# Aligning ScalarE's instruction stream to a 256-slot block in a two-layer expert kernel

## The chip, the cores and the metric

The kernel runs on one core of a Trainium2 chip. A core has five engines, each with an instruction stream of its own: TensorE (PE in the profile; PEld is its weight load), VectorE (DVE), ScalarE (ACT), GpSimd (POOL) and SyncE (SP). Data moves between the chip's memory and the core's buffers by DMA, over 16 DMA engines that all queues share. The metric is the time of one execution on the device, in microseconds (us); smaller is better.

## What is computed

Eight experts each apply two dense layers with bias to 256 rows of their own:

```python
n_experts, capacity, hidden, expert_hidden = 8, 256, 512, 2048
h = np.matmul(x, w1) + b1[:, np.newaxis, :]
h = np.maximum(h, 0)
return (np.matmul(h, w2) + b2[:, np.newaxis, :]).astype(np.float32)
```

All inputs and the output are 32-bit floats in the chip's memory. `w1` and `w2` together are 64 MiB of the data that must be read.

## The kernel before

The five engines' programs are written out by hand, one function for each, inside one critical section (L396): nothing there is reordered, and the only order between engines is by semaphores.

**Loads.** `run_gpsimd` issues the weight loads, which convert to 16-bit floats on the way: `w1` of an expert in one transfer of 2 MB as it lands (L173), `w2` likewise (L183), in halves for the last two experts. Three buffers stand for each (`NW = 3`), so a load of expert e + 3 waits until TensorE has done with expert e. `run_sync` issues the first loads of `x` and `b1` (L148, L150), turns the landing of weights into counts that TensorE can wait for (L155, L161), and issues the output of the last two experts. GpSimd also loads the small row `b2` (L187) and writes out the other results (L206).

**Compute.** TensorE walks `E + LAG = 11` steps in a loop over registers (L324). Step s does layer 1 of expert s (L344: 16 blocks j of 128 hidden columns, four matmuls each, into the four buffers `ph`) and layer 2 of expert s - 3 (L359 for the bias, L374 for 16 x 2 matmuls, into `po`). Its loop body is a few dozen instructions, run again and again.

**ScalarE** (`run_scalar`), by contrast, is straight code, one instruction for each piece of work, in this order:

- it waits until VectorE has transposed a pattern (L210, on `turned_steps`), copies four pieces of it into the identity matrix `ident` (L214, with a table load ahead of the first), which TensorE needs for its first transposes of `x` (L291);
- it waits for `x` of experts 2 and 3 and casts it (L218);
- it waits for the transposed `b1` and, for each expert and each j, applies bias and relu from `ph` to `hT` (L115, 128 in all); each one frees a `ph` buffer for TensorE (`ph_free`);
- from step 3 on, after the relus of a step, it copies results out of `po` (L127, 22 in all), which frees `po` for TensorE.

**VectorE** makes the transposes of `x` and `b1` (L235, L247, L266), casts the first two experts' `x`, copies what TensorE transposed (L241), and takes half of the copies from `po` of the last two experts.

At the end of the section the engines meet, SyncE issues the last output (L404) and waits for all of it. Ahead of the section each engine has a few instructions of the frame and one branch into the section (put down to L437).

Of the kernel before, what the change touches and what calls it, by code (L numbers as in the profile page):

```python
# [10 lines left out]
def kernel(  # L11
# [90 lines left out]
    def relu(e, j):  # L102
        rows = rows_of(e)
        R = x_rows(e)
        to, columns = hT[:, e % NH, j, :], ph[j % NPH][:, 0:T]
        if T // rows > R:
            m = T // rows // R
            to = to.rearrange("p (m r i) -> p m r i", m=m, r=R)
            columns = columns.rearrange("p (r i m) -> p m r i", r=R, m=m)
        else:  # L110
            m = R // (T // rows)
            to = to.rearrange("p (r i m) -> p r i m", m=m, i=rows // m)
            columns = columns.rearrange("p (m r i) -> p r i m", m=m, i=rows // m)
        at = j * B + e * nB + nB - 1
        return nc.scalar.activation(  # L115
            out=to, in_=columns, func=relu_of, bias=b1T[:, at : at + 1], scale=1.0)

    def result(e):

        if e in GROUP_OF:  # L120
            first, n = GROUP_OF[e]
            return grouped[first], (e - first) * (P // n), P // n, n
        return pair[e - (E - 2)], 0, P, 1

    def evict(e, lo, hi, k, copy):
        t, at, rows, split = result(e)
        return copy(  # L127
            out=t.rearrange("p (tb s) h -> p tb s h", s=split)[at : at + rows, lo:hi, k, :],
            in_=po[k * rows : (k + 1) * rows, e % 2, lo:hi, 0:H])

    def scalar_from(e):

        return 0 if e in GROUP_OF else nTB // 2
# [73 lines left out]
                s_out[first], 16)  # L207
    def run_scalar():
        a = nc.scalar
        a.wait_ge(turned_steps, 1)  # L210
        marks = {0: (ph_free, NPH), 1: (po_free_a, 1), nB - 1: (made_ident, 1)}
        for b in range(nB):
            part = slice(b * B, (b + 1) * B)
            ins = a.copy(out=ident[part, part], in_=steps_turned[part, :, 0])  # L214
            if b in marks:
                ins.then_inc(*marks[b])
        a.wait_ge(s_xg[2], 16)
        a.copy(out=x16[2], in_=x32[2]).then_inc(cast, 1)  # L218
        a.wait_ge(b1T_full, 1)
        for step in range(E + LAG):  # L220
            if step < E:
                for j in range(nJ):
                    a.wait_ge(ph_full, nJ * step + j + 1)
                    relu(step, j).then_inc(ph_free, 1)
            if step >= LAG:
                e = step - LAG
                a.wait_ge(po_full, ENDS * (e + 1))
                for k in range(result(e)[3]):
                    ins = evict(e, scalar_from(e), nTB, k, a.copy)
                ins.then_inc(po_free_a, 1)  # L230
# [165 lines left out]
    with tc.tile_critical(sync_engine=mybir.EngineType.SP, no_gpsimd_drain=True):  # L396
        run_gpsimd()
        run_sync()
        run_scalar()
        run_vector()  # L400
        run_tensor()
        nc.sync.wait_ge(po_free_a, 1 + E)
        nc.sync.wait_ge(po_free_d, 1 + E)
# [38 lines left out]
```

## Time and profile before

| what | value |
|---|---|
| median of 3 runs | 180.88 us (180.86 to 181.0) |
| the profiled execution's own time | 180.9 us |
| its span, from the first to the last instruction of the kernel | 179.1 us |
| around the span | 1.8 us |
| TensorE busy | 130.5 us (73%) |
| ScalarE busy | 82.0 us (46%), 156 instructions |
| VectorE busy | 40.2 us (22%) |
| data moved by the core's DMA | 40.98 MB, 229 GB/s |
| granted TensorE clock, mean | 0.964 of full speed |

How to read the views: a row of the timeline has a start, a length, the engine, the line and the operation, and how many instructions were merged (x4); in brackets stands the idle time of the engine before it and what ended it. A row of the groups has busy time and the mean of one instruction in ns, then idle time. A row of the DMA issues has how many there were, the size of each and the median time from issue to landing. A row of one source line has the shortest, median and longest duration in ns, then the first and the last start in us. In the queue part, q0 and q1 carry data and q14 carries the engines' program code. "issue" is time in which an engine waited for nothing that the profile shows. All times are counted from the span's start.

### The profile page before, as it was taken

The numbers are of one execution on the slowest core, as the hardware profiler recorded it, in microseconds if no ns is written. First come the engines' busy times: TensorE is split into PE (matmuls) and PEld (weight loads), VectorE is DVE, ScalarE is ACT, GpSimd is POOL, SyncE is SP. The second block draws the span as 40 slices with busy tenths as digits, with TensorE's granted clock in tenths as the row PEclk, the third lists the DMA queues.
The fourth block names the chain that finished last, engine by engine and source line by source line (L and its number), as shares of the span: only waits on it lengthen the run. The fifth ranks groups of instructions, "written<-read, shape, count | busy, mean of one in ns | idle before, by whom it ended". The sixth has DMA issues, their size and how long they took to land.

```text
span 179.1 us, 2849 instructions
## 1 busy us (share of the span) xinstructions
PE 130.5 (73%) x800; PEld 86.6 (48%) x800; DVE 40.2 (22%) x43; ACT 82.0 (46%) x156; POOL 13.2 (7%) x30
## 2 busy tenths in 40 slices
PE   0210695969879970899957995999669997999750
PEld 0200485858768430785436643774268433444310
DVE  0492299200000299992000000000000000001010
ACT  0500685877858126384089606890398212131010
POOL 7100003020010110001010001000200001002000
PEclk9999999999999998589999999699999999999996
DMA  5999999989989999998998999999899899999996
GB/s 194 267 249 302 212 198 234 231 179 234 236 187 220 238 209 201 234 223 187 234 234 183 227 234 198 212 234 220 190 234 234 183 227 205 210 225 209 318 454 252
DMA packets 3825, 40.98 MB, mean 229 GB/s; under 512 B 448, under 2 KB 464, under 8 KB 1008
## 3 DMA queue, kind: packets, MB, share of 16 engines
q0 software_dynamic: 3056, 37.76, 95.1%
q1 hardware_dynamic: 768, 3.21, 4.6%
q14 instruction: 1, 0.01, 0.0%
HBM read 71.39 MB, written 4.19 MB: 422 GB/s over the span
## 4 chain that ended last, share of the span: by engine, by line
DMA 44%; PE 23%; ACT 14%; another core or an unknown queue 11%; issue 4%; POOL 1%; SPq 0%; POOLq 0%
DMA w1sb<-in_w_dram 23%; PE ph L344 12%; DMA w2sb<-in_w_dram 12%; ACT hTsb L115 11%; PE po L374 10%; DMA b2sb<-in_b_dram 9%; ACT outg L127 2%; PE po L359 1%; POOL w1sb L173 0%; ACT pair L127 0%; POOL w2sb L183 0%; SPq L161 0%; SPq L155 0%; POOLq L437 0%
## 5 line engine op out<-in xcount | busy, mean ns | idle before, releaser
L344 PE MATMUL ph<-xTsb,w1sb 128*128 x512 | 67.7, 291 | 30.8 <-issue 15.1
L344 PEld LDWEIGHTS ph<-xTsb,w1sb 128*128 x512 | 58.6, 148 | 41.0 <-issue 38.5
L115 ACT ACTIVATE hTsb<-ph,b1T 128x256 f16<-128x256 f32 x128 | 56.7, 474 | 16.6 <-PE ph L344 16.2
L374 PE MATMUL po<-w2sb,hTsb 128*128 x256 | 56.8, 379 | 2.6 <-SPq L161 2.6
L374 PEld LDWEIGHTS po<-w2sb,hTsb 128*128 x256 | 25.0, 98 | 33.1 <-issue 5.7
L127 ACT COPY outg<-po 32x1024 f32<-32x1024 f32 (+1 forms) x20 | 20.1, 1005 | 43.7 <-PE po L374 43.5
L266 DVE STREAM_TRANSPOSE xTsb<-x 32x512 f16<-32x512 f16 (+1 forms) x32 | 31.0, 970 | 36.2 <-DMA x<-in_x_dram 29.0
L127 DVE COPY pair<-po 128x512 f32<-128x512 f32 x2 | 1.4, 692 | 88.5 <-PE po L374 88.5
L183 POOL DMA_DIRECT2D w2sb<-in_w_dram x10 | 5.3, 534 | 69.4 <-PE po L374 69.4
L173 POOL DMA_DIRECT2D w1sb<-in_w_dram x8 | 4.4, 551 | 66.6 <-PE ph L344 65.6
L291 PE MATMUL ph<-ident,x 128*128 128x128 f16 x16 | 1.9, 310 | 7.8 <-ACT ident L214 7.8
L127 ACT COPY pair<-po 128x512 f32<-128x512 f32 x2 | 1.2, 586 | 13.9 <-PE po L374 13.9
L218 ACT CAST x<-outg 128x2048 f16<-128x2048 f32 x1 | 1.9, 1899 | 11.5 <-DMA outg<-in_x_dram 11.5
L359 PE MATMUL po<-b2sb,ones 1*128 x16 | 4.8, 379 | 0.8 <-issue 0.7
L291 PEld LDWEIGHTS ph<-ident,x 128*128 128x128 f16 x16 | 1.6, 144 | 7.8 <-ACT ident L214 7.8
L247 DVE STREAM_TRANSPOSE b1T<-b1rows 32x512 f32<-32x512 f32 x4 | 4.1, 1020 | 0.1
L214 ACT ACT_TABLE_LOAD x1 | 1.3, 1283 | 5.4 <-DVE hTsb L235 5.4
L359 PEld LDWEIGHTS po<-b2sb,ones 1*128 1x128 f16 x16 | 1.4, 90 | 3.5 <-issue 3.2
L206 POOL DMA_DIRECT2D out_dram<-outg x2 | 1.1, 537 | 15.2 <-DMA w2sb<-in_w_dram 15.2
L235 DVE STREAM_TRANSPOSE hTsb<-hTsb 128x1024 f16<-128x1024 f16 x1 | 1.2, 1245 | 4.1 <-POOL hTsb L194 4.1
L241 DVE COPY xTsb<-ph 128x1024 f16<-128x1024 f16 x2 | 1.4, 692 | 2.5 <-PE ph L291 2.5
L238 DVE CAST x<-pair 128x1024 f16<-128x1024 f32 x2 | 1.3, 666 | 0.0
(11 smaller groups left out, 4.0 us busy)
## 6 DMA issues: line engine op xcount, KB each, us to landing
w1sb<-in_w_dram POOLq DMA_DIRECT2D x8, 2048.0 KB, 32.5
w2sb<-in_w_dram POOLq DMA_DIRECT2D x6, 2048.0 KB, 45.1
w2sb<-in_w_dram POOLq DMA_DIRECT2D x4, 1024.0 KB, 23.1
out_dram<-outg POOLq DMA_DIRECT2D x1, 2048.0 KB, 12.9
pair<-in_x_dram SPq DMA_DIRECT2D x2, 512.0 KB, 3.8
outg<-in_x_dram SPq DMA_DIRECT2D x1, 1024.0 KB, 16.9
x<-in_x_dram POOLq DMA_DIRECT2D x1, 1024.0 KB, 31.3
out_dram<-outg POOLq DMA_DIRECT2D x1, 1024.0 KB, 8.6
```

The lines of the kernel that those rows point to most:

```text
L115: return nc.scalar.activation(out=to, in_=columns, func=relu_of, bias=b1T[:, at : at + 1], scale=1.0)
L127: return copy(out=t.rearrange("p (tb s) h -> p tb s h", s=split)[at : at + rows, lo:hi, k, :], in_=po[k * rows : (k + 1) * rows, e % 2, lo ...
L173: g.dma_start(out=w1_sb[:, e % NW], in_=w1[e].rearrange("(p kc) m -> p kc m", kc=nKC)).then_inc(s_w1[e], 16)
L183: g.dma_start(out=w2_sb[:, e % NW, lo:hi], in_=src[:, lo:hi]).then_inc(s_w2[e, h], 16)
L218: a.copy(out=x16[2], in_=x32[2]).then_inc(cast, 1)
L241: v.tensor_copy(out=xT[:, e], in_=ph[2 + e].bitcast(fp16).rearrange("p (kc t) -> p kc t", kc=nKC),).then_inc(xT_full, 1)
L247: ins = v.transpose(out=b1T[b * B : (b + 1) * B, nB - 1 - b : nB - 1 - b + nJ * B], in_=b1_rows.rearrange("r (i j) -> r j i", j=nJ))
L266: ins = v.transpose(out=to[b * B : (b + 1) * B, :, :, half * B : (half + 1) * B], in_=src.rearrange("p r (i kc) -> p kc r i", kc=nKC))
L291: ins = t.transpose(out=pt[:, kc, r, :], in_=rows[:, kc, :], identity=ident)
L344: ins = t.matmul(out=ph[i][:, 0:T], lhsT=w1_cols(w1_j, i, kc), rhs=x_cols[kc], start=(kc == 0), stop=(kc == nKC - 1),)
L359: t.matmul(out=po_f[:, bass.ds(o + tb * 512, H)], lhsT=ones1, rhs=b2_sb[0:1, bass.ds(b_e, H)], start=True, stop=False, skip_group_check=True,)
L374: ins = t.matmul(out=po_f[:, bass.ds(o + tb * 512, H)], lhsT=hT_f[:, bass.ds(h_e + (j * T + tb * P), P)], rhs=w2_f[:, bass.ds(w_e + j * H, ...
```

## The change

One line is added at the head of ScalarE's program:

```diff
     def run_scalar():
         a = nc.scalar
+        a.addr_align(256, max_nops=0)
         a.wait_ge(turned_steps, 1)
         marks = {0: (ph_free, NPH), 1: (po_free_a, 1), nB - 1: (made_ident, 1)}
         for b in range(nB):
```

`addr_align` is a directive to the loader. When the program is loaded, the next instruction of that engine (here the wait at L210) is placed at a multiple of 256 instruction slots of the engine's stream, and the slots left free ahead of it are filled. With `max_nops=0` none of the filling is run: if there is any, its first slot is a branch to the placed instruction. The rest of ScalarE's program follows behind it, unchanged, and the other four engines' programs are the same.

## The prediction

> **What bounds the kernel now.** I read the page's head, its 40 slices and its queues first, to see which resource is full.
>
> ```profile
> span 179.1 us, 2849 instructions
> DMA  5999999989989999998998999999899899999996
> q0 software_dynamic: 3056, 37.76, 95.1%
> q1 hardware_dynamic: 768, 3.21, 4.6%
> q14 instruction: 1, 0.01, 0.0%
> ```
>
> The two data queues hold 95.1 + 4.6 = 99.7% of sixteen engines' time, and only the first and the last slices of the DMA line are below 8. The kernel streams its weights; compute runs beside that stream. The last line is the one this change is about: one packet of program code, printed as 0.01 MB, was read inside the span.
>
> Second, ScalarE's waits, since it is ScalarE's program that is laid out anew. The columns are: who waited for what, total us, times, longest.
>
> ```profile
> ACT outg L127 <- PE po L374: 43.5, 6, 7.3
> ACT hTsb L115 <- PE ph L344: 16.2, 29, 2.9
> ACT pair L127 <- PE po L374: 13.9, 2, 8.3
> ACT x L218 <- DMA outg<-in_x_dram: 11.5, 1, 11.5
> ACT L214 <- DVE hTsb L235: 5.4, 1, 5.4
> ```
>
> That is 90.5 us of idle time, and every entry names another engine or a load. No entry is put down to "issue", which is where an engine short of code would show. So nothing visible is there for a better layout to take away.
>
> Third, where that one code packet lies. The DMA view of the stretch from 46.3 to 46.8 us has it; the stretches before and after have no q14 row.
>
> ```profile
> q14 instruction: 1, 0.01, 4.0%
> ```
>
> Its time on an engine is 4.0% x 16 engines x 0.5 us = 0.32 us. Whose code is it? ScalarE is in new code at that time, while TensorE is in its third round of the loop at L344. VectorE, GpSimd and SyncE issue nothing new near it, so I take it for ScalarE's. The groups of ScalarE up to 46.39 us, and its two lone waits, tell how far it had come.
>
> ```profile
> L115 ACT ACTIVATE hTsb<-ph,b1T 128x256 f16<-128x256 f32 x43 | 19.3, 473 | 6.4 <-PE ph L344 6.3
> L218 ACT CAST x<-outg 128x2048 f16<-128x2048 f32 x1 | 1.9, 1899 | 11.5 <-DMA outg<-in_x_dram 11.5
> L214 ACT ACT_TABLE_LOAD x1 | 1.3, 1283 | 5.4 <-DVE hTsb L235 5.4
> L214 ACT COPY ident<-hTsb 32x32 f16<-32x32 f16 x4 | 1.0, 240 | 0.1
> L210 ACTq EVENT_SEMAPHORE  x1: 17/17/17, 5.3 to 5.3; - x1
> L223 ACTq EVENT_SEMAPHORE  x1: 17/17/17, 20.7 to 20.7; - x1
> ```
>
> 43 + 1 + 1 + 4 + 1 + 1 = 51 instructions of the section. So in the program of before a block edge lies some 51 slots into the section (an estimate: the sequencer may be a few ahead). What did crossing it cost? ScalarE's timeline on both sides, with an earlier row to compare:
>
> ```profile
> 33.46 1.78 ACT L115 ACTIVATE hTsb<-ph,b1T 128x256 f16<-128x256 f32 x4 [0.26 <-PE ph L344]
> 45.34 1.78 ACT L115 ACTIVATE hTsb<-ph,b1T 128x256 f16<-128x256 f32 x4 [0.28 <-PE ph L344]
> 47.39 1.78 ACT L115 ACTIVATE hTsb<-ph,b1T 128x256 f16<-128x256 f32 x4 [0.26 <-PE ph L344]
> ```
>
> Four relus take 1.78 us in all three rows, and the gaps are 0.26 to 0.28 us, ended by TensorE. The crossing cost nothing that can be seen.
>
> **The change part by part.** It adds a directive ahead of the wait at L210: filler up to the next multiple of 256 slots and, with no filler to be run, one branch over it. No wait, DMA or computation is added, removed or reordered; no other engine's code moves.
>
> *The branch.* ScalarE has one branch of its own in the trace, next to the others' here:
>
> ```profile
> L437 ACTq COMPARE_BRANCH  x1: 33/33/33, 0.8 to 0.8; - x1
> L437 PEldq COMPARE_BRANCH  x1: 174/174/174, 0.8 to 0.8; - x1
> 5.39 1.28 ACT L214 ACT_TABLE_LOAD   x1 [5.39 <-DVE hTsb L235]
> ```
>
> One more branch is 0.03 us by ScalarE's row, and 0.17 us by TensorE's as the far bound. It comes at 0.8 us, and ScalarE has nothing to do until VectorE's transpose ends at 5.3 us (the wait at L210). That wait hides 4.5 us, so the branch costs 0.
>
> *The code that it jumps to.* If the target has been read ahead, the jump is the branch alone. If it hasn't, ScalarE waits for a read. The trace of before has no such wait, so I bound it: from below 0.32 us, the code packet; from above the smallest loads' time to landing.
>
> ```profile
> pair<-in_x_dram SPq DMA_DIRECT2D x2, 512.0 KB, 3.8
> b1rows<-in_b_dram SPq DMA_DIRECT2D x1, 64.0 KB, 7.6
> b2sb<-in_b_dram POOLq DMA_DIRECT2D x1, 8.0 KB, 15.6
> 0.96 0.86 SPq L148 DMA_DIRECT2D pair<-in_x_dram  x2
> ```
>
> The first data is issued only at 0.96 us, so at 0.8 us a code read meets empty engines. The nearest row is the first one issued, 3.8 us for 512 KB; 0.8 + 3.8 = 4.6 us, still before 5.3. And there is a second cover behind the first:
>
> ```profile
> 7.76 1.89 PE L291 MATMUL ph<-ident,x 128*128 128x128 f16 x16 [7.76 <-ACT ident L214]
> 9.69 0.69 DVE L241 COPY xTsb<-ph 128x1024 f16<-128x1024 f16 x1 [0.16 <-PE ph L291]
> 19.23 1.90 ACT L218 CAST x<-outg 128x2048 f16<-128x2048 f32 x1 [11.53 <-DMA outg<-in_x_dram]
> 2.13 15.56 DMA b2sb<-in_b_dram
> 17.70 1.90 issue
> ```
>
> What ScalarE makes first (the identity) feeds TensorE's transposes and VectorE's copies, done at 9.69 + 0.69 = 10.4 us; in the chain that ended last TensorE then stands until the small load lands at 17.7 us. That leaves 7.3 us more. A stall at the jump would have to exceed 4.5 + 7.3 = 11.8 us to move the first matmul; I take 0.
>
> [...]
>
> *The code packet.* Where its edge moves from slot 51 to slot 0, the read of the block behind it moves from 46.4 us to about 0.8 us, from full engines to empty ones. All sixteen engines must finish each load, so at most its 0.32 us goes; an edge further on puts one back. I take 0, with -0.32 and +0.32 as ends.
>
> *The sum* against the profiled execution: 180.9 us = 179.1 of span + 1.8 around it, and the change 0 + 0 + 0. The median of the three times is 180.88, so the forecast is 180.9.
>
> **The rivals.** About 0.2% (0.36 us) is what a measurement of this kernel can tell from no change; a bare packet of 0.32 us stays below that.
>
> *A, forecast:* all of it is hidden, 180.9, within 180.6 to 181.2 by the packet's two ends. For it: waits without "issue", the crossing at 46.4 us for nothing, a cover of 11.8 us at the jump.
>
> *B, faster, in the end code.* What ScalarE runs after the last row of the profile lies in the 1.8 us around the span. The section has 8 + 128 + 22 = 158 instructions, five more close the program; from the old edge that end is 163 - 51 = 112 slots away, from the new one 163. If a block is shorter than 256 slots (0.01 MB is what one read brought), before has its next edge close behind the program's end, and the changed one hasn't. Bounds 0 and -1.8; I take half, -0.9: 180.0. Against it: nothing of that time is in any row.
>
> *C, slower, in the middle.* If blocks have 128 slots, the aligned section crosses an edge at slot 128. Which instruction is that? ScalarE's groups up to 119.0 us, and the rows that follow:
>
> ```profile
> L115 ACT ACTIVATE hTsb<-ph,b1T 128x256 f16<-128x256 f32 x108 | 48.0, 474 | 15.6 <-PE ph L344 15.4
> L127 ACT COPY outg<-po 32x1024 f32<-32x1024 f32 x12 | 12.1, 1005 | 22.0 <-PE po L374 21.9
> 115.20 3.56 ACT L115 ACTIVATE hTsb<-ph,b1T 128x256 f16<-128x256 f32 x8 [0.51 <-PE ph L344]
> 119.04 1.78 ACT L115 ACTIVATE hTsb<-ph,b1T 128x256 f16<-128x256 f32 x4 [0.29 <-PE ph L344]
> 128.11 4.05 ACT L127 COPY outg<-po 32x1024 f32<-32x1024 f32 x4 [7.29 <-PE po L374]
> 148.96 7.08 PE L374 MATMUL po<-w2sb,hTsb 128*128 x32 [1.37 <-SPq L161]
> 168.89 3.62 PE L374 MATMUL po<-w2sb,hTsb 128*128 x16 [1.21 <-SPq L161]
> ```
>
> 8 + 108 + 12 = 128: slot 128 is the first relu of the row at 119.04. ScalarE would ask for it at some 118.3 us, as the last of the eight before starts. The four relus (1.78 us) are in time if they end by 128.11, so a read may take 128.1 - 1.8 - 118.3 = 8.0 us for nothing. That is the point from which this decides: 7.6 us (the 64 KB row) is hidden; with 15.6 us (the 8 KB row) the copies start at 118.3 + 15.6 + 1.8 = 135.7, 7.6 us late. TensorE's two later idle times for data absorb 1.37 + 1.21, and 5.0 us are left: 185.9. Against it: the edge at 46.4 us was crossed under full engines without any of this.
>
> [...]
>
> *D, slower, in the end code:* B's mechanism with the sign turned, where the later end meets an edge or code not yet read that the old one didn't. Bounds 0 and +1.8, half of it: 181.8.
>
> *E, the directive changes nothing:* dropped, or the edge isn't where I count it. 180.9 again; the packet at 46.4 us would stay.
>
> **How the numbers follow.** A 0.47 and E 0.05 make 0.52 for within 0.2%. B gets 0.22: its place is possible by the slot count, but unseen. D gets 0.18, the same place with no slot count for it; C gets 0.08, since it needs short blocks and no reading ahead and over 8.0 us. Slower is 0.26. The time is A's, 180.9. The range leaves out C and the outer halves of B and D, 0.08 + 0.11 + 0.09 at most, part of which lies close to the ends: 180.0 to 181.8. A's own range is 180.6 to 181.2.
>
> **What would show it.** Right: the code packet is gone from 46.4 us and stands near 0.8 us; the wait at L210 still ends at 5.3 us, the first matmul at L344 starts at 19.6, and the last row of ScalarE (L127, pair) at 172.5. Jump stall: ScalarE's table load starts later than 5.4 us. C: a code packet near 118 us and a gap of over 8 us ahead of a relu. B or D: an unchanged span with another time around it. I am wrong if the span moves by over 0.36 us with ScalarE's waits as they are.

## The result and the profile after

The changed kernel takes 181.67 us in the median (181.46 at the least) against 181.02 us for the kernel before on the same chips. The ratio is 1.0033, with a 95% interval from 1.0022 to 1.0043: slower by 0.6 us. That lies inside the range of 180.0 to 181.8, but it is not the "within 0.2%" that I held likeliest, and it lies beyond the 181.2 at which my forecast A ended.

The profiled execution of the changed kernel took 181.46 us, 1.8 us more than its span, as before. So all of the difference is inside the span. Three rows of its page, the head and two queues:

```profile
span 179.7 us, 2850 instructions
q0 software_dynamic: 3056, 37.76, 94.8%
q14 instruction: 3, 0.02, 0.0%
```

The span is 0.6 us longer, one instruction was added (the branch), and there are three packets of program code where there was one. The DMA view of the stretches 0 to 5, 5 to 10 and 105 to 108 us has one each:

```profile
q14 instruction: 1, 0.01, 0.4%
```
```profile
q14 instruction: 1, 0.01, 0.4%
```
```profile
q14 instruction: 1, 0.01, 0.7%
```

In the trace they start at 2.09, 7.77 and 106.29 us, have 8192 bytes each and take 0.31 to 0.32 us. The one at 46.4 us is gone.

ScalarE itself is not held up by its code. Its branch, its first wait, and its waits in total:

```profile
L210 ACTq COMPARE_BRANCH  x1: 33/33/33, 0.9 to 0.9; - x1
L211 ACTq EVENT_SEMAPHORE  x1: 17/17/17, 5.3 to 5.3; - x1
ACT outg L127 <- PE po L375: 43.4, 6, 7.3
ACT hTsb L115 <- PE ph L345: 16.4, 30, 2.8
ACT pair L127 <- PE po L375: 13.9, 2, 8.3
ACT x L219 <- DMA outg<-in_x_dram: 11.7, 1, 11.7
ACT L215 <- DVE hTsb L236: 5.4, 1, 5.4
```

The wait still ends at 5.3 us, and no row says "issue"; the waits add up to 90.8 us, against 90.5 before. What is late is TensorE, and only where it waits for weights. Two rows of before that were not shown yet, then the timeline of the changed kernel:

```profile
19.60 0.65 PE L344 MATMUL ph<-xTsb,w1sb 128*128 x2 [9.95 <-issue]
110.91 9.40 PE L344 MATMUL ph<-xTsb,w1sb 128*128 x64 [1.90 <-SPq L155]
```
```profile
7.76 1.89 PE L292 MATMUL ph<-ident,x 128*128 128x128 f16 x16 [7.76 <-ACT ident L215]
19.81 0.43 PE L345 MATMUL ph<-xTsb,w1sb 128*128 x1 [10.16 <-issue]
111.45 2.88 PE L345 MATMUL ph<-xTsb,w1sb 128*128 x16 [1.96 <-SPq L155]
169.41 3.62 PE L375 MATMUL po<-w2sb,hTsb 128*128 x16 [1.21 <-SPq L161]
```

The first transposes, which need ScalarE's identity, start at 7.76 us as before. The first matmul on loaded weights is 0.21 us late (it waits for the small row `b2` too, which lands 0.22 us late); after the wait for `w1` of expert 6 (SPq L155) it is 0.54 us; the last 16 matmuls, behind the last half of `w2` (SPq L161), start at 169.41 instead of 168.89, 0.52 us. The delay came in two steps, the second after 106 us.

Each weight load raises its semaphore sixteen times, which I read as once for each DMA engine. The trace keeps these times. The latest of the sixteen, and how far it lies behind the second latest (us):

```
                      before                after
load               latest   behind      latest   behind
w1 of expert 0      17.02    0.03        17.25    0.24
b2                  17.70    0.03        17.92    0.22
w1 of expert 2      37.35    0.03        37.56    0.22
w1 of expert 3      47.55    0.50        47.26    0.24
w1 of expert 5      90.69    0.04        90.85    0.19
w1 of expert 6     110.02    0.02       110.56    0.56
w1 of expert 7     129.44    0.03       129.91    0.50
w2 of expert 7,
  second half      168.69    0.09       169.22    0.99
```

After the second packet one completion of the sixteen is 0.2 us behind all others, and after the third 0.5 to 0.6 us, up to the last load, where it is 1.0 us. The other fifteen are not late: the second latest of `w1` of expert 6 lands at 110.00 us in both kernels. TensorE follows the latest one: in both kernels its row at expert 6 starts 0.89 us after it. In the kernel before, the load under way at 46.4 us is late once, by 0.5 us, and then the lag is gone.

Why one lag goes and the other stays can be read from the packets. The trace gives each packet's start and length, and not its engine; but in these stretches (44 to 49 us before, 5 to 10 and 104 to 109 us after) every data packet of 8 KB or more starts within 0.02 us of the end of another packet. I take that one for its neighbour on the same engine, and find the neighbours of a code packet so. In the kernel before, the sixteen data packets under way at 46.38 us end between 46.385 and 46.753 us. The code packet stands behind the one that ends at 46.403: its engine was the second earliest. Behind the code its next data packet starts at 46.71, within those of the others (46.39 to 46.76). So 0.32 us of code used up a lead of 0.35 us, and no more. In the changed kernel the engine of the second code packet stands only 0.08 us ahead of the latest engine when it comes, and 0.23 us behind it afterwards. The data packet ahead of the third code packet ends at 106.31 us, when those of the other fifteen had ended by 106.09; the one behind it starts at 106.61, 0.54 us after the latest of the others. So the third packet fell on the engine that was late already.

That gave the theory to test. **Theory 1:** a code packet takes some 0.3 us of one DMA engine; the queues are full (94.8 + 4.6 = 99.4% of sixteen engines' time here), so that engine stays behind; a load has landed when its slowest engine is done, so every wait for weights ends later. **Theory 2:** the directive itself costs, by the branch or by where ScalarE's code now lies.

### The profile page after: what moved, and what is told of

It is laid out like the page before. It is cut to its first block, busy times and chain, and to the rows that moved or that the text cites. A ratio compares the mean times of both kernels' runs of the same rounds, so it can differ in the third digit from the quotient of the medians.

```text
span 179.7 us, 2850 instructions
## 1 busy us (share of the span) xinstructions
PE 130.9 (73%) x800; PEld 86.9 (48%) x800; DVE 40.2 (22%) x43; ACT 82.1 (46%) x156; POOL 13.2 (7%) x30
## 3 DMA queue, kind: packets, MB, share of 16 engines
q0 software_dynamic: 3056, 37.76, 94.8%
## 4 chain that ended last, share of the span: by engine, by line
DMA 38%; PE 34%; ACT 14%; DVE 6%; issue 3%; POOL 1%; SPq 0%; POOLq 0%
PE po L375 18%; DMA x<-in_x_dram 17%; PE ph L345 15%; DMA w2sb<-in_w_dram 12%; DMA b2sb<-in_b_dram 9%; ACT hTsb L115 7%; ACT outg L127 7%; DVE xTsb L267 6%; PE po L360 1%; POOL w1sb L173 1%; POOL w2sb L183 1%; ACT pair L127 0%; POOLq L438 0%; SPq L161 0%; SPq L397 0%
```

## The experiments

### The same alignment on VectorE, ScalarE left alone

```diff
         v = nc.vector
+        v.addr_align(256, max_nops=0)
         v.wait_ge(memsets, 4)
```

> VectorE aligned to 256 slots, ScalarE as before. VectorE has about 50 instructions in the section, so no second edge inside. Theory 1: a code packet or two in the first 10 us, on whichever DMA engine reads VectorE's code, one engine's landings late from then on by some 0.2 us: +0.2 us (0 to 0.4), and ScalarE's packet at 46.4 us still there. Theory 2 (ScalarE's own layout): 0.0 us.

Measured: ratio 1.0040 (1.0025 to 1.0055), 0.7 us slower. The code packets are at 1.97 and 8.41 us, and one that I take for ScalarE's own at 49.1. The queue in the whole run and in the first 5 us, TensorE's last row, and ScalarE's longest wait for TensorE:

```profile
q14 instruction: 3, 0.02, 0.1%
q14 instruction: 1, 0.01, 1.7%
170.00 3.62 PE L375 MATMUL po<-w2sb,hTsb 128*128 x16 [1.22 <-SPq L161]
ACT outg L127 <- PE po L375: 43.1, 6, 7.3
```

ScalarE's program is that of before, and the loss is there, above the 0.0 to 0.4 that I expected. The first packet was longer than I reckoned: 1.7% of sixteen engines' 5 us is 1.36 us, not 0.32. One completion lies 1.0 us behind the second latest at `w1` of expert 1 and 0.83 to 0.88 from 57 to 165 us. Theory 2 fails as far as it speaks of ScalarE.

### Four undivided loads of 8 KB

The main part of the edit; `probe` is a new buffer, and at the end SyncE waits for `s_probe`.

```diff
                 s.sem_inc(w1_in, 1)
+                if 1 <= step <= 4:
+                    s.dma_start(
+                        out=probe[step - 1 : step, 0:2039],
+                        in_=x[step].rearrange("p h -> (p h)").rearrange("(o f) -> o f", o=1)[:, 0:2039],
+                    ).then_inc(s_probe, 16)
```

> No alignment anywhere. SyncE issues four loads of 8156 bytes (2039 numbers, which don't divide into 16 pieces) at the landing of the weights of experts 1 to 4, into a buffer that nothing reads. Theory 1: if each is one packet on one and the same engine, that engine is 4 x 0.3 us behind less the up to 0.35 us by which the earliest engine leads: +0.6 to +1.2 us. Rival (the loss is in ScalarE's program, not in the engines' balance): 0.0 us, as 32 KB of 41 MB is 0.14 us at 229 GB/s at most.

Measured: ratio 1.0055 (1.0040 to 1.0071), 0.94 us slower. The DMA issues, the code queue and TensorE's last row:

```profile
probe<-in_x_dram SPq DMA_DIRECT2D x4, 8.0 KB
q14 instruction: 1, 0.01, 0.0%
170.05 3.62 PE L381 MATMUL po<-w2sb,hTsb 128*128 x16 [1.33 <-SPq L168]
```

One code packet, as before, no alignment, and the same kind of loss: in the trace each load is one packet of 8156 bytes that takes 0.32 us, and one completion falls behind by 0.69 us after the third and 0.99 after the fourth.

### The same with 8192 bytes

```diff
-                        out=probe[step - 1 : step, 0:2039],
+                        out=probe[step - 1 : step, 0:2048],
```

(and the same on the source)

> The same four loads with 2048 numbers (8192 bytes), which divide into 16 pieces, so that each engine gets 512 bytes of each. Theory 1: every engine has the same small addition, 0.0 to +0.15 us, clearly less than with the undivided loads. Rival to theory 1 (bytes or issuing as such cost the time): the same as with the undivided loads.

Measured: ratio 1.0056 (1.0041 to 1.0070). The expectation failed in its premise, that such a load is divided over the engines: no run shows that, and in the trace each of these loads, one row of one partition, is again one packet, of 8192 bytes. So it is a repetition of the run before, and gave the same. The control had to be built in another way.

### The same bytes in 16 rows

```diff
+                    at = (step - 1) * 128
+                    s.dma_start(
+                        out=probe[:, at : at + 128],
+                        in_=x[step].rearrange("p h -> (p h)").rearrange("(q f) -> q f", f=128)[0:16, :],
+                    ).then_inc(s_probe, 16)
```

> As the four loads before, 8192 bytes each at the same places, but into 16 rows of 512 bytes, so that each of the 16 engines gets one row of each load. Theory 1 (a packet on one engine makes that engine late, and every load waits for the latest): no engine falls behind the others, 0.0 to +0.25 us over before, where the undivided loads gave +0.95. Rival (the extra bytes, or SyncE's issuing, cost the time): +0.95 again.

Measured: ratio 1.0002 (0.9988 to 1.0016).

```profile
probe<-in_x_dram SPq DMA_DIRECT2D x4, 8.0 KB, 6.0
169.05 3.62 PE L382 MATMUL po<-w2sb,hTsb 128*128 x16 [0.96 <-SPq L169]
```

The same bytes in the same number of loads, issued at the same places of the program, and no loss that can be measured. The four loads add 128 packets to the 768 of q1, where the undivided ones added 8. The last matmuls start at 169.05, a full 1.0 us before those of the undivided loads, and no completion is more than 0.23 us behind the second latest in the loads. It is not the bytes and not the issuing: it is that all 8192 bytes of a load went out as one packet, on what I take for one engine.

### No branch: the filler is run

```diff
         a = nc.scalar
+        a.addr_align(256, max_nops=255)
```

> ScalarE aligned to 256 as in the change, but the filler is run instead of branched over (up to 255 instructions without work, inside the 4.5 us for which ScalarE waits anyway if there are about 60; beyond that they eat into the 7 us behind it). No taken branch, so the code is read in sequence. Theory 1: the time goes with the code packets inside the span: with the same three as in the change +0.65 us, with two about +0.3 to +0.5, with one 0.0 to +0.3. Theory 2 (the taken branch itself is what costs): 0.0 us even with three packets.

Measured: ratio 1.0046 (1.0033 to 1.0059), 0.8 us slower without the branch over the filler. The filler at L210, ScalarE's first work, the code queue, and two rows of TensorE:

```profile
L210 ACTq NOP  x188: 14/14/14, 0.9 to 8.5; - x188
9.01 1.28 ACT L215 ACT_TABLE_LOAD   x1 [9.01 <-issue]
q14 instruction: 3, 0.02, 0.0%
19.86 0.44 PE L345 MATMUL ph<-xTsb,w1sb 128*128 x1 [6.58 <-issue]
169.79 3.62 PE L375 MATMUL po<-w2sb,hTsb 128*128 x16 [1.54 <-SPq L161]
```

188 slots of filler put the section, without alignment, at slot 256 - 188 = 68 (an estimate). The filler's starts are 0.04 us apart but for one gap of 0.34 us after the 60th, at slot 68 + 60 = 128. So I take a block here to have 128 slots (an estimate); the old edge then lies 60 slots into the section, not 51, and the change skips a whole edge. (No code packet is read near that gap, at 3.2 us: the trace doesn't say what the gap is.) There are three packets again (7.5, 12.1 and 105.1 us), and the loss is there. Theory 2's branch is out.

ScalarE also began 3.6 us late (9.01 instead of 5.39), and the first matmul came at 19.86, against 19.81 in the changed kernel: the second cover is real.

### Aligned with a branch, but with one edge

```diff
         a = nc.scalar
+        a.addr_align(128, offset=84, max_nops=0)
```

> ScalarE's section starts at slot 84 of a block of 128: the run filler showed that it starts at slot 68 without alignment, so the branch skips 16 slots and stays in the loaded block. The edge comes 16 instructions earlier in the section and there is only one. Theory 1 (the number of code packets inside the full stream): one packet, near 38 us instead of 46, so 0.0 to +0.25 us over before, although it is aligned with a branch. Theory 2 (directive, branch or moved code as such): as the change, +0.65 us or more.

Measured: ratio 1.0017 (0.9999 to 1.0035), not to be told from no change.

```profile
q14 instruction: 2, 0.01, 0.0%
169.28 3.62 PE L375 MATMUL po<-w2sb,hTsb 128*128 x16 [1.63 <-SPq L161]
```

One of the two packets has 56 bytes, of a kind that the other runs have just ahead of the span; the only one of 8 KB is at 36.6 us. The latest completion of the load under way lies 0.45 us behind the second latest, that of the next one 0.02. A branch is run at 0.9 us here too. In the profiled execution, at 181.46 us one of the longer ones, the last matmuls are 0.39 us late all the same; there the two latest completions of the last load are 0.01 us apart, so it is not one engine.

### The same with two edges

```diff
         a = nc.scalar
+        a.addr_align(128, offset=100, max_nops=0)
```

> The same with slot 100: 32 slots skipped inside the loaded block, an edge at instruction 28 of the section and a second one at 156. Theory 1: two packets, near 27 and near 140 us, so one more than before and than with slot 84: +0.2 to +0.6 us over before. Theory 2 (directive, branch or moved code as such): the same as with slot 84.

Measured: ratio 1.0012 (1.0001 to 1.0023), 0.2 us, at the low end of what was expected and not apart from the run with slot 84. The two packets are where they were placed, and TensorE's last row has the second one's trace:

```profile
q14 instruction: 2, 0.02, 0.0%
169.23 3.62 PE L375 MATMUL po<-w2sb,hTsb 128*128 x16 [1.12 <-SPq L161]
```

They start at 27.1 and 136.4 us. The first makes one load 0.53 us late, after which the lag is 0.02; behind the second it stays at 0.30 to 0.37, and is 0.72 at the last load. Both runs are aligned and branch. With slot 100 the loss ends at 0.42 us, below the 0.6 us of the change; with slot 84 the median is 0.1 us above before, but the interval reaches to 0.63. Blocks of 128 put the edges 44, 28 and 156 slots into the section; the packets, expected near 38, 27 and 140 us, came at 36.6, 27.1 and 136.4.

### Aligned to 128

```diff
         a = nc.scalar
+        a.addr_align(128, max_nops=0)
```

> ScalarE aligned to 128 slots instead of 256, same branch over the filler. Theory 1 (each code packet takes some 0.3 us of one DMA engine, and every load waits for its slowest engine): if the next multiple of 128 is the block that the sequencer reads anyway, the read at 2.1 us is gone and two code packets are left (near 8 and near 106 us), so half of the loss or less: +0.1 to +0.4 us over before. If 128 and 256 are the same place, three packets and +0.65 us. Theory 2 (the branch and ScalarE's own place in the block cost the time): branch and alignment are there as with 256, so +0.65 us, whatever the packets.

Measured: ratio 1.0042 (1.0027 to 1.0057), 0.6 us by median, 0.8 by the ratio, and more than I expected of two packets.

```profile
q14 instruction: 2, 0.02, 0.1%
```

They start at 1.93 and 105.3 us. The lag is 0.44 us from the first load on, for most loads, and 0.70 to 0.78 after the second packet. So the number of packets alone doesn't give the loss: here the first one left a lag, in the two runs before it left none. The trace shows a difference: the first packet took 1.30 us here, longer than the 0.35 us of lead, and all those of the two runs before 0.32. Both long ones, here and in the run on VectorE, begin just ahead of the first data packets (1.98 and 1.97 us); why the one of the change, at 2.09 us among them, took 0.32 us is not shown. By itself this run would also fit theory 2.

### Alignment where the loads are not waited for

```diff
+            part = nKC if e < NW else nKC // 2
             g.dma_start(
-                out=w1_sb[:, e % NW], in_=w1[e].rearrange("(p kc) m -> p kc m", kc=nKC)
+                out=w1_sb[:, e % NW, 0:part],
+                in_=w1[e].rearrange("(p kc) m -> p kc m", kc=nKC)[:, 0:part],
...
+                if e >= NW:
+                    hi = (lo + hi) // 2
```

> Left out: the second half of the weights of experts 3 to 7 (older data in the buffers is used instead), so 20 MiB fewer are read and the queue no longer sets the pace; ScalarE is not aligned. Both theories: several us faster than before, bound by TensorE. It is the base for the next kernel.

> The same with half of the weights of experts 3 to 7 left out, and ScalarE aligned to 256 as in the change. Theory 1: a load that lands 0.2 to 0.5 us late is no longer waited for once the queue runs ahead, so only the first loads (the packet near 2 and 8 us) can still cost: 0.0 to +0.3 us against the same kernel without the alignment. Theory 2 (branch and layout of ScalarE): +0.65 us, as with full loads, since ScalarE's program is the same.

Measured against the kernel before: 0.9705 (0.9675 to 0.9735) without the alignment, 0.9652 (0.9613 to 0.9691) with it. TensorE's waits in the one without:

```profile
PE ph L348 <- issue: 17.1, 8, 9.9
PE ph L348 <- ACT hTsb L115: 10.6, 4, 2.7
PE ph L295 <- ACT ident L218: 7.8, 1, 7.8
PE po L363 <- issue: 0.9, 5, 0.2
```

No row of SPq is left: TensorE no longer waits for a count of landed weights. There the alignment is not slower; the difference of the ratios is -0.0053, some 1.0 us in its favour, with about 0.9 us either way. By the means of all six runs of each it is 0.7 us, with some 1.3 either way, so that the +0.65 us of theory 2 is only just outside. This is weak evidence beside the runs above. It doesn't show a gain: the times of both scatter over 2 to 3 us, and what moves them was not looked into.

## Why the prediction was right or wrong

**The range held by luck.** Its upper end, 181.8, came from D, a mechanism in the end code that did not occur; A's own range ended at 181.2. The prediction also named a sign of being wrong, and it came: the span moved by 0.6 us, more than 0.36, with ScalarE's waits nearly as they were. Three of its signs of being right failed too. The first code packet stands at 2.09 us and not near 0.8, the first matmul starts at 19.81 instead of 19.6, and ScalarE's last row at 173.07 instead of 172.5.

**The branch: right.** 0.03 us at 0.9 us, hidden by the wait that still ends at 5.3.

**The code that it jumps to: right.** A packet was read at 2.09 us, which I take for the target of the jump; the wait at L211 still ended at 5.3 us, behind the first cover, and the run with filler showed the second cover at work over 3.6 us.

**The code packet: wrong, and this is the step that failed.** I took one packet moved from full engines to empty ones, 0 us with 0.32 us either way. It was three packets. I read them as the target of a jump over a whole edge (2.09 us), the block behind it (7.77 us), and a third for the edge at slot 128 of the section (106.29 us); the trace doesn't name a packet's block. The price of a packet, 0.32 us of one of sixteen engines, was right here; the sum was not, since the lag stayed and added up: 0.2 us behind the second packet, 0.5 to 0.6 behind the third. Three packets are 0.95 us; less the lead of 0.35 us that this engine had in the kernel before, 0.6 us is left (an estimate). Measured were 0.53 us at the landing of the last load and 0.6 us of span. I had written that all sixteen engines must finish each load, and then bounded the term by a single packet.

**What misled:** I judged the packet of before by ScalarE's rows alone, where it cost nothing. For the loads it was nearly free as well (the lag was 0.03 us again at the next load), but only because its engine had a lead of 0.35 us to lose. The runs with slots 84 and 100 show the same for their first packet, and 0.3 us left by the next.

**B and D, the end code: wrong.** The time around the span is 1.8 us in both kernels. **C: the place was right, the price was not.** The edge at slot 128 has its packet, at 106.3 us and not near 118, when ScalarE had begun 112 instructions of the section, so by this count it was read some 16 ahead (an estimate). ScalarE doesn't stand for it; it is the loads that land late. Blocks of 256 slots are shown by no run; blocks of 128 put the packets of the runs with slots 84 and 100 near 38, 27 and 140 us, and they came at 36.6, 27.1 and 136.4. **E: wrong,** the packet of 46.4 us is gone.

The chances had 0.26 for slower, all of it from mechanisms that did not occur. That the sign was not excluded was right; its reason was not.

## What to carry to other kernels

This kernel's DMA queues are full: 99.4% of sixteen engines' time. There, three blocks of code of 0.32 us each, or four undivided rows of 8 KB, also 0.32 us each, made the loads behind them land late once their engine's lead (0.35 us in the kernel before) was used up, and the kernel 0.6 and 0.94 us slower; the bytes of the four in 16 rows each cost nothing that could be measured. In a kernel with queues as full, add up how long such packets hold one engine, not their bytes, and spread what can be spread over 16 rows. Before aligning straight code, count the edges that the new position gives and the blocks that the jump skips: here an alignment that added two reads of code cost 0.6 us, although the waits of the engine that runs the code came to 90.8 us against 90.5.

## What the runs showed of the hardware that was not expected

- The places of the code packets of 8192 bytes inside the span fit blocks of 128 slots (an estimate, from the filler's count and the packets of the runs with slots 84 and 100). Most took 0.31 to 0.32 us; of the four that began near the first data, at about 2 us, one did too, and the others took 0.61, 1.30 and 1.36 us. The filler's starts, 0.04 us apart otherwise, have one gap of 0.34 us, after the 60th, where 128 slots would put an edge; the trace doesn't say what it is.
- In these runs a DMA of one row of 8156 or 8192 bytes went out as one packet of data; four of them made the kernel 0.94 to 1.0 us slower, and the same bytes in 16 rows 0.0 us (ratio 1.0002).
- The lag that packets left in the changed kernel lasted to the end of the run: 0.17 to 0.24 us from the second packet on, 0.48 to 0.58 at the loads of weights from the third on, 0.99 at the last of them. The first one was absorbed within the next load in three runs (a lag of 0.45 to 0.53 us, then 0.02 to 0.03); in the kernel before, its engine had been 0.35 us ahead of the latest. The second one with slot 100 left 0.30 to 0.37 us, and one of 1.30 us in the run aligned to 128 left 0.44. Which of the sixteen engines it is, and why that packet took 1.30 us, stays open.
